# Scores of the two strided attention groups with the keys' high and low parts side by side in one 256-column operand, and one more step at the second strided group's first value projection

## The chip, the cores and the metric

The kernel runs on one core of one Trainium2 chip. The metric is the device time of one execution in microseconds. Four of the core's engines matter here: TensorE (PE in the profile; its weight loads have a row of their own, PEld), VectorE (DVE), ScalarE (ACT) and the DMA queues, of which the ACT queue carries a few small transfers that this change touches.

## What is computed

One layer of a bidirectional encoder on 512 tokens of width 1024, in float32: a SwiGLU feed-forward half step, a token-mixing block, and a second feed-forward half step, each normalised before and after. The change lies in the mixing block, in the branch with twelve heads of 64 features in three groups. Each group is a banded attention over tokens that lie `dilation` apart; the three groups' outputs are then mixed per token and head by a softmax over their log-sum-exps:

```python
DIL_PAIRS = ((128, 1), (512, 4), (2048, 16))
for g, (window, dilation) in enumerate(DIL_PAIRS):
    half = window // (2 * dilation)
    o, lse = _dilated_attention(q[:, :, g], k[:, :, g], v[:, :, g], dilation, half, sl)
    outs.append(o)
    lses.append(lse)
alpha = jax.nn.softmax(jnp.stack(lses, axis=0), axis=0)
o = jnp.stack(outs, axis=0) * alpha[..., None]
```

Inside a group the scores are q·k/8 minus a slope times the distance, and minus infinity outside the band. Group 0 has dilation 1; groups 1 and 2 (dilation 4 and 16) are the strided ones, called far groups in the code. The kernel walks both in the order "token modulo 4", so that 512 tokens become four tiles of 128, and a tile's queries meet only the keys of the same tile.

## The kernel before

**Numbers in two parts.** Nearly every operand of TensorE is split into a high part (a copy of type fp32r, by ScalarE) and a low part (the rest, by VectorE): the helper `split`, lines 111 to 113. A product is then three matmuls, high by high, high by low and low by high (`mm3`, lines 202 to 205). For the scores only 64 features are contracted, so the query's two parts stand one above the other in the 128 partitions (rows `own` high, rows `other` low, line 914), and the key's high part and low part each stand twice, once for each half. Two matmuls then give the whole score: the query tile by `kh`, and the query tile by `kl` added onto it in PSUM.

**`qk_parts`** (line 905) makes those operands for the two heads of a pair from two PSUM banks, `pq` and `pk`: two units of 512 columns for the keys, `kh` and `kl`, with a ScalarE copy and a VectorE subtraction of 512 columns each, and one copy of each into the other 64 partitions.

**`scores`** (line 1025) serves all groups before the change. For group 0 and the neighbourhood branch the windows are wide (256 keys to a query tile), two tiles to a PSUM bank. For the far groups they are narrow (128 keys to a tile, four tiles in one bank), eight matmuls of 128 columns to a head. VectorE then adds the bias table and takes the row minimum of the negated score in one instruction for each tile (line 1041, `tensor_tensor_reduce`), and ScalarE takes the exponential and its sum (line 1046), both with an accumulated result that a second short instruction reads out.

**The order of the work.** TensorE's stream is built by hand. Long projections (24 matmuls) are emitted one after another, and between them a queue `pend` of short pieces of attention is worked off: `step(n)` takes n of them (lines 197 to 200). In the stretch of the change `pend` holds the scores of the far heads, written (g, h) below, and then `joint(1)`. The projections there are: the last pair of query and key projections; `v_far(1)` and `v_far(2)`, two value projections each, copied out of PSUM by ScalarE (line 971); then `v_far(1)`'s eight transposes (line 979); then `v_near`, four groups of 24 matmuls of 256 columns (line 957); then `v_far(2)`'s eight transposes; then sixteen gate projections of 512 columns (line 1294). Before the change a step stands after each of the four value projections, after every second group of transposes, and after each group of `v_near`.

**What hangs on the last scores.** After head 3 of a group its row minima and sums go to DRAM (line 1243, a DMA on the ACT queue). `joint(g)` (line 1221) reads those of all three groups back (line 1224) and works out the mixing weights in about ten short VectorE instructions (lines 1227 to 1236) with one exponential on ScalarE between them (line 1231). `g_tr(g, h)` scales the probabilities by these weights (line 1057) and TensorE transposes them (line 1069). The first of these, `g_tr(1, 0)`, is taken behind the second gate projection.

**The other traffic of VectorE and ScalarE.** Each projection takes one weight piece of 128 by 1024 (two parts) and makes the next one but four be converted: a cast on ScalarE (line 112) and a subtraction on VectorE (line 113). They stand in the same in-order queues as the attention's work. The order within each engine is set by a scheduler at build time, except in stretches that are pinned; the gates' sigmoid and the exponential need different tables on ScalarE, and a table load stands in its queue at each switch.

Of the kernel before, what the change touches and what calls it, by code (L numbers as in the profile page):

```python
# [13 lines left out]
F32R = mybir.dt.float32r  # L14
BF16 = mybir.dt.bfloat16
AF = mybir.ActivationFunctionType
ALU = mybir.AluOpType
# [3 lines left out]
P = 128  # L21
# [24 lines left out]
def block_kernel(ctx, tc, x, gains, weights, rpb_near, rpb_all, alibi0, alibi12, out):  # L46
    nc = tc.nc
# [12 lines left out]
    def unit(dt=F32, name="u"):  # L60
        return up.tile([P, 512], dt, tag="u", name=name)
# [6 lines left out]
    def bank(name="ps"):  # L68
        return pp.tile([P, 512], F32, tag="ps", name=name)
# [41 lines left out]
    def split(hi, lo, src):  # L111
        nc.scalar.copy(hi, src)  # L112
        nc.vector.tensor_tensor(lo, src, hi.bitcast(F32), op=ALU.subtract)  # L113
# [83 lines left out]
    def step(n=1):  # L197
        for _ in range(n):
            if pend:
                pend.popleft()()  # L200
# [671 lines left out]
    def seen(kind, ap):  # L872

        if kind == "na":
            return ap.rearrange("p (r c) -> p c r", r=8)
        if kind == 0:
            return ap
        return ap.rearrange("p (i c) -> p c i", c=4)

    def order_k(kind, ap):  # L880
        if kind == "na":
            return [(slice(0, 128), ap.rearrange("p (r b c) -> p b c r", r=8, b=8)[:, 0:8:7]),
                    (slice(128, 512), ap.rearrange("p (r c) -> p c r", r=8)[:, 8:56])]
        if kind == 0:
            return [(slice(0, 128), ap.rearrange("p (b c) -> p b c", b=8)[:, 0:8:7]),
                    (slice(128, 512), ap[:, 64:448])]
        return [(slice(0, 512), seen(kind, ap))]
# [9 lines left out]
    def shaped(dst, view):  # L897
        sh = view.shape
        if len(sh) == 2:
            return dst  # L900
        if len(sh) == 3:
            return dst.rearrange("p (a b) -> p a b", a=sh[1])
        return dst.rearrange("p (a b c) -> p a b c", a=sh[1], b=sh[2])

    def qk_parts(kind, pq, pk):


        heads = []
        for par in range(2):
            own = slice(par * 64, par * 64 + 64)  # L910
            other = slice(64 - par * 64, 128 - par * 64)
            q, kh, kl = unit(F32R), unit(F32R), unit(F32R)
            v = seen(kind, pq[own])
            qo, qx = shaped(q[own], v), shaped(q[other], v)
            nc.scalar.mul(qo, v, 0.125)
            nc.vector.scalar_tensor_tensor(qx, v, 0.125, qo.bitcast(F32), op0=ALU.mult, op1=ALU.subtract)
            for cols, v in order_k(kind, pk[own]):
                split(shaped(kh[own, cols], v), shaped(kl[own, cols], v), v)
            nc.vector.tensor_copy(kh[other], kh[own].bitcast(F32))
            nc.scalar.copy(kl[other], kl[own].bitcast(F32))  # L920
            heads.append((q, kh, kl))
        return heads
# [39 lines left out]
    def v_far(g):  # L962


        feats = []
        for _ in range(2):
            o = bank()
            proj_into(o, take())
            u = unit(name="vt")
            v = seen(g, o)  # L970
            nc.scalar.copy(shaped(u, v), v)
            feats.append(u)
            step()
        yield
        vv = []
        for n in range(4):
            ps = bank()
            for i, u in enumerate(feats):
                nc.tensor.transpose(ps[:, i * P:(i + 1) * P], u[:, n * P:(n + 1) * P], ident)
            vv.append(v_parts(ps[:, :256]))  # L980
            if n % 2:
                step()
        yield vv

    def v_proj_na():
# [29 lines left out]
                vv[i].append(v_parts(acc[n][:, i * 256:(i + 1) * 256]))  # L1015
        yield vv

    def windows(wide, kT, i):
        if not wide:
            return kT[:, i * P:(i + 1) * P]  # L1020
        if i < 3:
            return kT[:, i * P:i * P + 256]
        return kT.rearrange("p (b c) -> p b c", b=4)[:, 0:4:3]

    def scores(wide, parts, table, st, h):

        q, kh, kl = parts
        w = 256 if wide else 128
        per = 512 // w
        prob = []  # L1030
        for b in range(NT // per):
            ps = bank()
            p = unit()
            for i in range(b * per, (b + 1) * per):
                o = (i - b * per) * w
                cols = slice(i * P, (i + 1) * P)
                nc.tensor.matmul(ps[:, o:o + w], q[:, cols], windows(wide, kh, i), start=True, stop=False)
                nc.tensor.matmul(ps[:, o:o + w], q[:, cols], windows(wide, kl, i), start=False, stop=True)
            for i in range(b * per, (b + 1) * per):
                o = (i - b * per) * w  # L1040
                nc.vector.tensor_tensor_reduce(
                    out=p[:, o:o + w], in0=ps[:, o:o + w], in1=table(i), scale=-1.0, scalar=3.0e38,
                    op0=ALU.add, op1=ALU.min, accum_out=st[:, i, h, 0:1])
            for i in range(b * per, (b + 1) * per):
                o = (i - b * per) * w
                nc.scalar.activation(p[:, o:o + w], p[:, o:o + w], AF.Exp, bias=st[:, i, h, 0:1],
                                     scale=-1.0, accum_out=st[:, i, h, 1:2])
            prob.append(p)
        return prob
# [106 lines left out]
    def mixing(g):  # L1156
        o_parts = [None] * 10
        hold = {}

        def table_of(us, h):  # L1160
            def f(i):
                s = (h % 2) * 3 + (0 if i == 0 else 2 if i == 3 else 1)
                return us[s // 2][:, (s % 2) * 256:(s % 2) * 256 + 256]
            return f
# [20 lines left out]
        na_tab = [[] for _ in range(4)]  # L1185
# [2 lines left out]

        def na_sc(parts, h):
            s4 = sp.tile([P, 4, 1, 2], F32, tag="nast", name="nast", bufs=4)  # L1190
            pr = scores(True, parts[h % 2], table_of(na_tab[h // 2], h), s4, 0)
            rc = sp.tile([P, 4], F32, tag="narc", name="narc", bufs=4)
            nc.vector.reciprocal(rc, s4[:, :, 0, 1])
            scale_probs(True, pr, lambda i: rc[:, i:i + 1])
            hold["p", h] = pr
# [19 lines left out]
        g_tab = {0: [], 1: [], 2: [], 3: []}  # L1215
        st_u = unit(name="st")
        st = [st_u[:, g * 32:g * 32 + 32].rearrange("p (t h c) -> p t h c", t=4, h=4) for g in range(3)]
# [19 lines left out]
            scl[g] = s  # L1237

        def g_sc(g, parts, h):
            tab = table_of(g_tab[h // 2], h) if g == 0 else lambda i: g_tab[g + 1][0][:, h * P:(h + 1) * P]  # L1240
            hold["p", g, h] = scores(g == 0, parts[h % 2], tab, st[g], h)
            if h == 3:
                nc.scalar.dma_start(st_views[g][:, :, 8 * g:8 * g + 8], st[g].rearrange("p t h c -> p t (h c)"))

# [63 lines left out]
        parts = {}  # L1308
        duos = [[None] * 2 for _ in range(2)]
        n0 = total - 3 * NF - NK  # L1310
        o = Blocks(n0, 1, duos)
# [210 lines left out]
    part = small("ms0")  # L1522
# [168 lines left out]
```

## Time and profile before

| | us |
|---|---|
| median of 3 runs (lowest, highest) | 1084.52 (1083.33, 1084.96) |
| the profiled execution | 1084.06 |
| its span, first to last instruction | 1081.9 |
| busy in that span: TensorE | 1074.0 (99%) |
| TensorE's weight loads | 968.4 (90%) |
| VectorE | 834.3 (77%) |
| ScalarE | 658.5 (61%) |

How to read it: the profiled execution has its own time, 2.2 us longer than its span (1084.06 - 1081.9), and 0.5 us under the median of the runs. In the views by time (the timeline), a row has its start, its duration, the engine, the line, the operation with the tile that it writes and those that it reads, its shape, and in square brackets the idle time of the engine before it with what ended it. TensorE's durations overlap: two matmuls that start 0.23 us apart are shown with 0.39 us each, so the price of a matmul in a stream is the distance from its start to the start of the next.

### The profile page before, as it was taken

How to read it: one execution, taken by the hardware profiler on the slowest of the kernel's cores; microseconds unless marked ns; L12 is line 12 of the kernel's file. 1: busy time of each engine (PE TensorE's matmuls, PEld its weight loads, DVE VectorE, ACT ScalarE, POOL GpSimd, SP SyncE). 2: the span in 40 equal slices, each digit the busy share in tenths (PEclk: the TensorE clock that was granted, in tenths of full speed). 3: DMA queues.
4: the chain of work that ended last, by engine and by line, in shares of the span. 5: the costliest groups of instructions: out<-in, count | busy, mean ns of one | idle time of the engine just before them, and what ended most of it. 6: DMA issues, size and time to landing. Idle time of an engine off the chain costs nothing.

```text
span 1081.9 us, 18434 instructions
## 1 busy us (share of the span) xinstructions
PE 1074.0 (99%) x6691; PEld 968.4 (90%) x6691; DVE 834.3 (77%) x1568; ACT 658.5 (61%) x1339; POOL 178.2 (16%) x247
## 2 busy tenths in 40 slices
PE   9999999999999999999999999999999999999997
PEld 7899999998888988888988888889899999998886
DVE  8987777778997679876467654777988777778985
ACT  7645555565784767767656651366656555565762
POOL 3111122014334000000000001133302111104301
PEclk9999999999999999999999999999999999999999
DMA  9888898569993453422232239665928777759962
GB/s 324 194 207 223 218 237 219 143 169 289 236 282 96 128 182 120 136 84 79 74 100 82 78 96 311 159 115 193 292 76 211 193 167 188 197 180 240 217 206 78
DMA packets 95725, 189.82 MB, mean 175 GB/s; under 512 B 24081, under 2 KB 26641, under 8 KB 95634
## 3 DMA queue, kind: packets, MB, share of 16 engines
q1 hardware_dynamic: 68320, 134.18, 37.3%
q0 software_dynamic: 24624, 54.01, 27.7%
q8 instruction: 52, 0.85, 0.3%
q10 hardware_dynamic: 2690, 0.46, 0.2%
q14 instruction: 39, 0.32, 0.1%
HBM read 183.58 MB, written 7.58 MB: 177 GB/s over the span
## 4 chain that ended last, share of the span: by engine, by line
PE 96%; DVE 1%; ACT 1%; DMA 1%; issue 0%; POOL 0%; DVEq 0%; ACTq 0%; POOLq 0%
PE q L203 11%; PE q L204 11%; PE q L205 11%; PE ps L203 11%; PE ps L204 11%; PE ps L205 11%; PE p L203 4%; PE p L204 4%; PE p L205 4%; PE r L205 3%; PE r L203 3%; PE r L204 3%; PE c L204 2%; PE c L205 2%; PE c L203 2%; PE ps L1069 1%
## 5 line engine op out<-in xcount | busy, mean ns | idle before, releaser
L113 DVE TENSOR_TENSOR w<-raw,w 128x512 fp32r<-128x512 f32 (+1 forms) x136 | 122.9, 909 | 70.0 <-ACT w L112 69.8
L112 ACT CAST w<-raw 128x512 fp32r<-128x512 f32 (+1 forms) x136 | 107.9, 801 | 84.9 <-PE ps L204 42.2
L203 PE MATMUL ps<-hn,w 128*128 128x512 f32 (+1 forms) x408 | 155.5, 381 | 0.2
L204 PE MATMUL ps<-hn,w 128*128 128x512 f32 (+1 forms) x408 | 153.2, 376 | 0.2 <-DVE hn L340 0.2
L205 PE MATMUL ps<-hn,w 128*128 128x512 f32 (+1 forms) x408 | 153.2, 375 | 0.0
L112 ACT CAST w<-t 128x512 fp32r<-128x512 f32 x160 | 97.1, 619 | 52.3 <-DVE t L402 29.3
L113 DVE TENSOR_TENSOR w<-t,w 128x512 fp32r<-128x512 f32 x160 | 109.2, 689 | 23.6 <-ACT w L112 20.9
L203 PE MATMUL p<-v,w 128*128 128x256 f32 x320 | 90.6, 283 | 0.0
L204 PE MATMUL p<-v,w 128*128 128x256 f32 x320 | 90.5, 283 | 0.0
L203 PE MATMUL q<-v,w 128*128 128x256 f32 x320 | 90.5, 283 | 0.0
L204 PE MATMUL q<-v,w 128*128 128x256 f32 x320 | 90.4, 283 | 0.0
L205 PE MATMUL p<-v,w 128*128 128x256 f32 x320 | 90.2, 283 | 0.0
L205 PE MATMUL q<-v,w 128*128 128x256 f32 x320 | 89.9, 283 | 0.0
L205 PEld LDWEIGHTS ps<-hn,w 128*128 128x128 f32 x408 | 76.8, 188 | 14.0
L203 PEld LDWEIGHTS ps<-hn,w 128*128 128x128 f32 x408 | 76.9, 189 | 13.2 <-ACT hn L339 0.4
L204 PEld LDWEIGHTS ps<-hn,w 128*128 128x128 f32 x408 | 77.0, 189 | 13.0 <-DVE hn L340 0.5
L396 POOL DMA_DIRECT2D t<-in_weights_dram x40 | 35.0, 874 | 287.0 <-DMA t<-in_weights_dram 124.0
L205 PE MATMUL q<-hn,w 128*128 128x256 f32 x288 | 81.5, 283 | 0.0
L204 PE MATMUL q<-hn,w 128*128 128x256 f32 x288 | 81.5, 283 | 0.0
L203 PE MATMUL q<-hn,w 128*128 128x256 f32 x288 | 81.3, 283 | 0.0
L203 PE MATMUL q<-w,a 128*128 128x512 f32 x192 | 75.0, 391 | 0.2 <-DVE part L851 0.2
L204 PE MATMUL q<-w,a 128*128 128x512 f32 x192 | 74.7, 389 | 0.0
(283 smaller groups left out, 3020.6 us busy)
## 6 DMA issues: line engine op xcount, KB each, us to landing
raw<-in_weights_dram SPq DMA_DIRECT2D x90, 512.0 KB
t<-in_weights_dram SPq DMA_DIRECT2D x88, 256.0 KB
t<-in_weights_dram POOLq DMA_DIRECT2D x80, 256.0 KB, 5.5
w<-in_weights_dram SPq DMA_DIRECT2D x40, 256.0 KB
rows<-in_weights_dram SPq DMA_DIRECT2D x32, 256.0 KB
w<-in_weights_dram POOLq DMA_DIRECT2D x32, 256.0 KB, 6.6
tb<-in_weights_dram POOLq DMA_DIRECT2D x12, 512.0 KB, 8.0
rows<-in_weights_dram POOLq DMA_DIRECT2D x24, 256.0 KB, 10.2
```

What stands on the lines that cost most here:

```text
L112: nc.scalar.copy(hi, src)
L113: nc.vector.tensor_tensor(lo, src, hi.bitcast(F32), op=ALU.subtract)
L203: nc.tensor.matmul(o, sh, mh, start=start, stop=False, **kw)
L204: nc.tensor.matmul(o, sh, ml, start=False, stop=False, **kw)
L205: nc.tensor.matmul(o, sl, mh, start=False, stop=stop, **kw)
L396: nc.gpsimd.dma_start(t1, weights[gate][:, :512], accum_op=ALU.add)
L1069: nc.tensor.transpose(ps[:, i * P:(i + 1) * P], s, ident)
```

## The change

Three things, all in the mixing block:

1. For the far groups `qk_parts` no longer makes one unit of high parts and one of low parts. Each of the two key units now holds two tiles' 256 high columns and then the same tiles' 256 low columns. So the copy and the subtraction of 512 columns become two copies and two subtractions of 256.
2. A new function, `scores_narrow`, replaces `scores` for the far groups. A query tile meets its 128 high and 128 low key columns in one matmul of 256 columns, taken as two runs of 128 that lie 256 columns apart. The two products lie side by side in PSUM instead of being added there. A head fills two PSUM banks with two matmuls each. VectorE first adds the low products of two tiles to the bias table (`low`, 128 by 256), and the row minimum then adds the high product to that.
3. The steps: `v_far(2)` takes two steps behind its first projection instead of one, and the steps between the transposes of both `v_far` are gone.

```diff
             q, kh, kl = unit(F32R, "q"), unit(F32R, "k"), unit(F32R, "k")
...
-            for cols, v in order_k(kind, pk[own]):
-                split(shaped(kh[own, cols], v), shaped(kl[own, cols], v), v)
+            if kind in (1, 2):
+                v = seen(kind, pk[own])
+                for i, u in enumerate((kh, kl)):
+                    part = v[:, 2 * i:2 * i + 2]
+                    split(shaped(u[own, :256], part), shaped(u[own, 256:], part), part)
+            else:
+                for cols, v in order_k(kind, pk[own]):
+                    split(shaped(kh[own, cols], v), shaped(kl[own, cols], v), v)
...
-        for _ in range(2):
+        for i in range(2):
             o = bank()
             proj_into(o, take())
...
-            step()
+            step(2 if (g, i) == (2, 0) else 1)
...
             vv.append(v_parts(ps[:, :256]))
-            if n % 2:
-                step()
...
+    def scores_narrow(parts, table, st, h):
+
+        q, ks = parts[0], parts[1:]
+        p = unit()
+        for b in range(2):
+            ps = bank()
+            for i in range(2):
+                k = ks[b].rearrange("p (s n t) -> p n s t", s=2, n=2)[:, i]
+                nc.tensor.matmul(ps[:, i * 256:(i + 1) * 256], q[:, (2 * b + i) * P:(2 * b + i + 1) * P], k,
+                                 start=True, stop=True)
+            low = unit(name="low")
+            o = ps.rearrange("p (n s t) -> p n s t", n=2, s=2)
+            nc.vector.tensor_tensor(low[:, :256].rearrange("p (n t) -> p n t", n=2), o[:, :, 1],
+                                    table.unsqueeze(1).to_broadcast([P, 2, P]), op=ALU.add)
+            for n in range(2):
+                i = 2 * b + n
+                nc.vector.tensor_tensor_reduce(
+                    out=p[:, i * P:(i + 1) * P], in0=o[:, n, 0], in1=low[:, n * P:(n + 1) * P], scale=-1.0,
+                    scalar=3.0e38, op0=ALU.add, op1=ALU.min, accum_out=st[:, i, h, 0:1])
+            for i in (2 * b, 2 * b + 1):
+                s = slice(i * P, (i + 1) * P)
+                nc.scalar.activation(p[:, s], p[:, s], AF.Exp, bias=st[:, i, h, 0:1], scale=-1.0,
+                                     accum_out=st[:, i, h, 1:2])
+        return [p]
...
-            hold["p", g, h] = scores(g == 0, parts[h % 2], tab, st[g], h)
+            if g == 0:
+                hold["p", g, h] = scores(parts[h % 2], table_of(g_tab[h // 2], h), st[g], h)
+            else:
+                hold["p", g, h] = scores_narrow(parts[h % 2], g_tab[g + 1][0][:, h * P:(h + 1) * P], st[g], h)
```

The lines below `qk_parts` have other numbers in the changed kernel: the scores' product is L1035, the sum with the table L1039, the row minimum L1043, its exponential L1048, the value transposes L985, the transfers of `stats` and `joint` L1271 and L1250, joint's instructions L1253 to L1262, the scaling L1083, the probabilities' transposes L1095 and the sigmoid L1324.

The order of the instructions on each engine, at three places. First TensorE around `v_far(1)`'s transposes. Before, head (1,3) stands between the two halves of the transposes (L979), as eight products of 128 columns:

```order
L979 MATMUL ps<-ident,vt 128x128 x4
L1037 MATMUL ps<-u 128x128
L1038 MATMUL ps<-u 128x128
L1037 MATMUL ps<-u 128x128
L1038 MATMUL ps<-u 128x128
L1037 MATMUL ps<-u 128x128
L1038 MATMUL ps<-u 128x128
L1037 MATMUL ps<-u 128x128
L1038 MATMUL ps<-u 128x128
L979 MATMUL ps<-ident,vt 128x128 x4
```

Now the head (1,3) stands ahead of all eight transposes, as four products, and the first matmuls of `v_near` follow at once:

```order
L205 MATMUL ps<-hn,w 128x512
L1035 MATMUL ps<-k,q 128x256 x4
L985 MATMUL ps<-ident,vt 128x128 x8
L203 MATMUL ps<-w,hn 128x256
L204 MATMUL ps<-w,hn 128x256
```

Heads (1,1) and (1,2) now follow each other behind `v_far(2)`'s first projection, (2,0) to (2,3) stand behind the first to the fourth group of `v_near` (before, (2,3) stood behind the third), and `joint(1)` comes after `v_far(2)`'s transposes. Of the first four probability transposes, before all ahead of the third gate, TensorE now does one ahead of that gate and three behind its nineteenth matmul.

Second, ScalarE from the last exponentials to the first of `joint`. `w<-raw` is the cast of a weight piece, `u<-ps` a part of the values, `stats` and `joint` are the transfers to and from DRAM. Before:

```order
L1046 ACTIVATE u,st<-u,st 128x128 x4
L112 CAST w<-raw 128x1024
L1243 DMA stats<-st 512x1x8
L112 CAST u<-ps 128x4x64
L112 CAST w<-raw 128x1024
L1224 DMA joint<-stats 128x96
L112 CAST u<-ps 128x4x64 x4
L1231 ACTIVATE joint<-joint 128x48
```

Now, from the last two exponentials of head (2,2) on (the `x4` are those of head (2,3)):

```order
L1048 ACTIVATE u,st<-u,st 128x128 x2
L112 CAST u<-ps 128x4x64
L112 CAST w<-raw 128x1024
L112 CAST u<-ps 128x4x64 x4
L1048 ACTIVATE u,st<-u,st 128x128 x4
L1271 DMA stats<-st 512x1x8
L112 CAST w<-raw 128x1024
L1250 DMA joint<-stats 128x96
L1324 ACT_TABLE_LOAD
L1324 ACTIVATE sig<-ps 128x512
L1257 ACT_TABLE_LOAD
L1257 ACTIVATE joint<-joint 128x48
```

The casts of a weight piece and of five value parts, which stood behind the last exponentials, now stand ahead of them, and the first gate's sigmoid with two table loads has come between the reading of `joint` and its exponential.

Third, VectorE at head (2,3). `ISA u,st` is the row minimum, `ISA st` its short second instruction. Before:

```order
L1041 ISA u,st<-ps,table 128x128
L1041 ISA st 128x1
L113 TENSOR_TENSOR w<-raw,w 128x1024
L113 TENSOR_TENSOR u<-ps,u 128x4x64
L113 TENSOR_TENSOR w<-raw,w 128x1024
L113 TENSOR_TENSOR u<-ps,u 128x4x64 x2
L1227 TENSOR_TENSOR joint<-joint 128x16
```

Now, from the second sum with the table on:

```order
L1039 TENSOR_TENSOR low<-ps,table 128x256
L113 TENSOR_TENSOR w<-raw,w 128x1024
L113 TENSOR_TENSOR u<-ps,u 128x4x64 x2
L1043 ISA u,st<-ps,low 128x128
L1043 ISA st 128x1
L1043 ISA u,st<-ps,low 128x128
L1043 ISA st 128x1
L113 TENSOR_TENSOR u<-ps,u 128x4x64 x2
L113 TENSOR_TENSOR w<-raw,w 128x1024
L1253 TENSOR_TENSOR joint<-joint 128x16
```

A weight subtraction and two value parts now stand between the head's last `low` and its last two row minima, and another weight subtraction ahead of `joint`'s first instruction; one more, not shown, stands ahead of the head's first `low`. SyncE's and GpSimd's orders are the same as before.

More of the change, by code (lines that the diff above doesn't have):

```diff
@@ L911, in qk_parts @@
             other = slice(64 - par * 64, 128 - par * 64)
-            q, kh, kl = unit(F32R), unit(F32R), unit(F32R)
+            q, kh, kl = unit(F32R, "q"), unit(F32R, "k"), unit(F32R, "k")
             v = seen(kind, pq[own])
@@ L1016, in v_proj_na, with windows @@
         yield vv
-    def windows(wide, kT, i):
-        if not wide:
-            return kT[:, i * P:(i + 1) * P]
+    def windows(kT, i):
         if i < 3:
@@ L1023, in windows, with scores @@
         return kT.rearrange("p (b c) -> p b c", b=4)[:, 0:4:3]
-    def scores(wide, parts, table, st, h):
+    def scores_narrow(parts, table, st, h):
[21 more added lines that the diff above has]
+        return [p]
+    def scores(parts, table, st, h):
         q, kh, kl = parts
-        w = 256 if wide else 128
-        per = 512 // w
+        w, per = 256, 2
         prob = []
@@ L1036, in scores @@
                 cols = slice(i * P, (i + 1) * P)
-                nc.tensor.matmul(ps[:, o:o + w], q[:, cols], windows(wide, kh, i), start=True, stop=False)
-                nc.tensor.matmul(ps[:, o:o + w], q[:, cols], windows(wide, kl, i), start=False, stop=True)
+                nc.tensor.matmul(ps[:, o:o + w], q[:, cols], windows(kh, i), start=True, stop=False)
+                nc.tensor.matmul(ps[:, o:o + w], q[:, cols], windows(kl, i), start=False, stop=True)
             for i in range(b * per, (b + 1) * per):
@@ L1190, in na_sc @@
             s4 = sp.tile([P, 4, 1, 2], F32, tag="nast", name="nast", bufs=4)
-            pr = scores(True, parts[h % 2], table_of(na_tab[h // 2], h), s4, 0)
+            pr = scores(parts[h % 2], table_of(na_tab[h // 2], h), s4, 0)
             rc = sp.tile([P, 4], F32, tag="narc", name="narc", bufs=4)
@@ L1239, in g_sc @@
         def g_sc(g, parts, h):
-            tab = table_of(g_tab[h // 2], h) if g == 0 else lambda i: g_tab[g + 1][0][:, h * P:(h + 1) * P]
-            hold["p", g, h] = scores(g == 0, parts[h % 2], tab, st[g], h)
+            if g == 0:
+                hold["p", g, h] = scores(parts[h % 2], table_of(g_tab[h // 2], h), st[g], h)
+            else:
+                hold["p", g, h] = scores_narrow(parts[h % 2], g_tab[g + 1][0][:, h * P:(h + 1) * P], st[g], h)
             if h == 3:
```

## Prediction

> **What bounds the kernel now.** I read the page's head and its chain first, then the waits of TensorE, then the windows around the change, last the timelines. The page:
>
> ```profile
> span 1081.9 us, 18434 instructions
> ...
> PE 1074.0 (99%) x6691; PEld 968.4 (90%) x6691; DVE 834.3 (77%) x1568; ACT 658.5 (61%) x1339; POOL 178.2 (16%) x247
> ...
> PEclk9999999999999999999999999999999999999999
> ...
> PE 96%; DVE 1%; ACT 1%; DMA 1%; issue 0%; POOL 0%; DVEq 0%; ACTq 0%; POOLq 0%
> ```
>
> TensorE is busy 99% of the span, the chain that ended last is TensorE's for 96%, and the clock is full in every slice. All waits of TensorE on other engines are three rows, 1.6 us together:
>
> ```profile
> PE warm L1470 <- DVE idle L1435: 1.2, 1, 1.2
> PE ps L204 <- DVE hn L340: 0.2, 1, 0.2
> PE q L203 <- DVE part L851: 0.2, 1, 0.2
> ```
>
> None stands at the attention. In the window that holds two of the strided heads TensorE is full too, while VectorE is busy 7.38 of 10 us (columns: TensorE, weight loads, VectorE, ScalarE, GpSimd, clock, DMA share, GB/s):
>
> ```profile
> 530.00:540.00 10.00, 10.00 (x88) 10.00 (x86) 7.38 (x47) 9.35 (x47) 0.00 (x0) 1.00 0.20 57
> ```
>
> So a shorter TensorE stream shortens the time, as long as no new wait arises. Two sums decide: what TensorE saves, and how late `joint(1)` becomes.
>
> **TensorE's saving.** A wide head (eight products of 256 columns) and a narrow head (eight of 128), each with the long matmul behind it:
>
> ```profile
> 508.35 0.28 PE L1037 MATMUL ps<-u 128*128 128x256 f32 x1
> ...
> 509.07 0.28 PE L1037 MATMUL ps<-u 128*128 128x256 f32 x1
> 509.19 0.28 PE L1038 MATMUL ps<-u 128*128 128x256 f32 x1
> 509.31 0.40 PE L203 MATMUL ps<-hn,w 128*128 128x512 f32 x1
> 509.54 0.40 PE L204 MATMUL ps<-hn,w 128*128 128x512 f32 x1
> ...
> 514.77 0.22 PE L1037 MATMUL ps<-u 128*128 128x128 f32 x1
> ...
> 515.62 0.45 PE L203 MATMUL ps<-hn,w 128*128 128x512 f32 x1
> 515.91 0.40 PE L204 MATMUL ps<-hn,w 128*128 128x512 f32 x1
> ```
>
> Eight products of 128 take 514.77 to 515.62, 0.85 us (0.11 each), and the next long matmul holds TensorE 0.29 (515.62 to 515.91) where behind the wide head it holds it 0.23 (509.31 to 509.54): 0.91 us in all. Eight products of 256 take 508.35 to 509.31, 0.96 us: 0.12 each, hardly more than one of 128. So four of 256 should take 0.48, and a head saves 0.43. Eight heads: 3.4 us. The after-effect of 0.06 was not paid by (1,2) and (1,3), which transposes followed, so 3.3. The new operand is read in two runs of 128 columns; the price I use already covers that, since the last window of the wide head (509.07 to 509.19, 0.12) is also read in two pieces (both ends: 0.12, or 0.24 if each run cost a product of its own).
>
> A rule on this: the Trainium skill, "TensorE: Matmul & The Clock Gate", section "Back-to-back issue gap", gives some 0.081 us per matmul of 128 columns in a stream with weight loads and N/2.4 + 2.5 ns, 0.109 at 256, for an isolated one. By these figures eight heads would save 8 x (8 x 0.081 - 4 x 0.109) = 1.7 us, not 3.4. The row of 128 columns (0.11) disagrees with the page, that of 256 (0.12) is near it; I go by the rows.
>
> The steps also break the first four probability transposes in two, 1 and 3, with one more switch from a long product to transposes and back. Before, one such group stands here (with the end of head (2,3), the first product behind it, and when the probability transposes are first asked for):
>
> ```profile
> 542.32 0.33 PE L203 MATMUL ps<-w,u 128*128 128x256 f32 x1
> ...
> 545.25 1.04 PE L979 MATMUL ps<-ident,vt 128*128 128x128 f32 x8
> 546.04 0.47 PE L203 MATMUL ps<-hn,w 128*128 128x512 f32 x1
> 546.35 0.39 PE L204 MATMUL ps<-hn,w 128*128 128x512 f32 x1
> ...
> 557.03 0.60 PE L1069 MATMUL ps<-ident,u 128*128 128x128 f32 x4
> ```
>
> The product behind transposes holds TensorE 0.31 (546.04 to 546.35) instead of 0.23: 0.1 lost. Net saving without waits: 3.2 us.
>
> **What is hidden.** VectorE gets sixteen `low` instructions. No row shows one; the nearest is a VectorE instruction on 128x256 read from PSUM (546.62 below), 0.33 from start to start; ends 0.28, a row minimum of half the width, and 1.0, nearly that of 1024 columns. I take 0.33, that of the same size: 16 x 0.33 = 5.3 us of VectorE beside a TensorE that is full while VectorE has 2.6 of 10 us idle. Cost nothing, except in the chain below. The eight copies and eight subtractions of 512 columns that become sixteen and sixteen of 256 add some fixed parts, 0.1 to 0.2 us each, on engines with idle time there; nothing if the next heads' operands are still a projection ahead, as they were.
>
> **`joint(1)`, the new wait.** Here the change uses up spare time. Before, the chain from (2,3)'s products (542.32) to the first scaled probabilities ends at 551.8 to 552.1, and TensorE asks for them at 557.03: about 5 us spare. Now (2,3) stands 24 products later, and the queues of VectorE and ScalarE that it passes through have moved too. VectorE's rows (start and duration; the bracket is the idle time before):
>
> ```profile
> 538.75 0.29 DVE L1041 CUSTOM_DVE_ANT_0 u<-ps,table 128x128 f32<-128x128 f32 x1 [1.66 <-PE ps L1038]
> ...
> 538.96 0.28 DVE L1041 CUSTOM_DVE_ANT_0 u<-ps,table 128x128 f32<-128x128 f32 x1
> ...
> 546.62 0.42 DVE L113 TENSOR_TENSOR u<-ps,u 128x256 fp32r<-128x256 f32 x1
> 546.95 1.22 DVE L113 TENSOR_TENSOR w<-raw,w 128x1024 fp32r<-128x1024 f32 x1
> 548.08 0.75 DVE L113 TENSOR_TENSOR u<-ps,u 128x256 fp32r<-128x256 f32 x2
> 549.02 0.18 DVE L1227 TENSOR_TENSOR joint<-joint 128x16 f32<-128x16 f32 x1 [0.18 <-DMA joint<-stats]
> ...
> 549.78 0.17 DVE L1228 TENSOR_TENSOR joint<-joint 128x16 f32<-128x16 f32 x1
> ...
> 550.63 0.21 DVE L1232 TENSOR_TENSOR joint<-joint 128x48 f32<-128x48 f32 x1 [0.31 <-ACT joint L1231]
> ...
> 551.79 0.88 DVE L1057 TENSOR_SCALAR u<-u,joint 128x128 f32<-128x128 f32 x4
> ```
>
> and ScalarE's with its DMA issues:
>
> ```profile
> 544.02 0.39 ACT L1046 ACTIVATE u<-u,st 128x128 f32<-128x128 f32 x1
> ...
> 544.41 1.03 ACT L112 CAST w<-raw 128x1024 fp32r<-128x1024 f32 x1
> 544.53 0.52 ACTq L1243 DMA_DIRECT2D stats<-st  x1
> 545.45 0.37 ACT L112 CAST u<-ps 128x256 fp32r<-128x256 f32 x1
> 545.71 1.05 ACT L112 CAST w<-raw 128x1024 fp32r<-128x1024 f32 x1
> 546.64 0.37 ACTq L1224 DMA_DIRECT2D joint<-stats  x1
> ...
> 550.35 0.24 ACT L1231 ACTIVATE joint<-joint 128x48 f32<-128x48 f32 x1 [2.10 <-DVE joint L1230]
> ...
> 552.63 1.28 ACT L1296 ACT_TABLE_LOAD   x1
> 553.93 0.60 ACT L1296 ACTIVATE sig<-ps 128x512 f32<-128x512 f32 x1
> ```
>
> From start to start: value part 0.33 (546.62 to 546.95), weight subtraction 1.13 (to 548.08), row minimum 0.21, exponential 0.39, weight cast 1.04 (544.41 to 545.45), value cast 0.26. I add these in the new order, with zero where the first `low` of head (2,2) starts, which is when its first two products are done (0.12 + 0.28 = 0.40 after its start):
>
> - TensorE: `v_near`'s last group starts at 0.48 - 0.40 = 0.1 and takes 542.32 to 545.25, 2.9; (2,3) 0.5, its first two products done at about 3.4; eight transposes 0.8 (545.25 to 546.04); two gates 11.0 (546.04 to 557.03). The scaled probabilities are asked for at 15.2.
> - VectorE, (2,2): `low` 0, value part, minima 0.7 and 0.9, `low` 1.1, minima to 2.1. ScalarE: two exponentials from 1.1, weight cast 1.8 to 2.9, two exponentials, value cast, weight cast 3.8 to 4.9, value casts 4.8 to 5.9.
> - VectorE then waits for the first cast: subtraction 2.9 to 4.1, so (2,3)'s first `low` starts at 4.1 instead of 3.4. Value part 4.4, minima 4.7 and 4.9, `low` 5.2, weight subtraction 5.5, two value parts 6.6 and 7.0, the last minima 7.3 and 7.5, done at 7.9.
> - ScalarE: exponentials 7.7 and 8.1, done with their read-out at 8.7; `stats` is issued; the read of `joint` follows 2.1 later (544.53 to 546.64), 10.8; `joint`'s first instruction 2.4 after that (546.64 to 549.02), 13.2.
> - The exponential of `joint` stood 1.33 behind it (549.02 to 550.35), with two value parts (0.67) between, which are now ahead: 0.7 to 0.8, so 14.0. In its queue the sigmoid with two table loads starts behind the read's issue: 10.9 + 1.3 + 0.6 + 1.3 = 14.1, level with it.
> - From the exponential to the scaling 1.44 (550.35 to 551.79): 15.5, and the first scaled tile 0.2 to 0.3 later, 15.8.
>
> Asked for at 15.2, there at 15.8: TensorE waits 0.6 us. If VectorE took the minima of (2,3) at once when its products are done, the chain would be 2 us or more shorter and nothing would be waited for; if the queues run another 0.6 late, which is as much as one cast that slips behind a value part or two, it is 1.2. So 0 to 1.2, and I take the sum, 0.6. Other probability transposes come behind this one and find their tiles scaled 0.2 apart.
>
> Total: 3.2 - 0.6 = 2.6 us less. The profiled execution took 1084.06 us (2.2 outside its span): 1081.5. The median shown is 0.5 higher, so on its scale 1081.9.
>
> **Rivals.**
>
> - *The wait is wholly covered.* The scheduler's order hides the weight subtractions or the DMA pair comes back faster. For it: the sum misses by only 0.6 of 15. Against: three in-order queues have to be on time. Full saving, 3.3: 1081.2.
> - *The chain is 1.5 to 3 us late.* Each stop (the cast, the DMA pair, the table loads) may slip, and the level pair at 14.1 leaves no slack. The saving shrinks to between 1.2 and 0: 1083.3 to 1084.5. Against: the durations are rows of the same engines, a few us away.
> - *Slower: `low` is dear.* It reads PSUM in two pieces and a table repeated by a stride of nothing. Per group of `v_near` (24 x 0.12 + 0.48 = 3.4 us) VectorE has two `low`, four minima, a value part and a weight subtraction: 0.66 + 0.84 + 0.33 + 1.13 = 3.0. From a `low` of 0.85 us VectorE is the slower engine; at 1.0 it is 4.3, 0.9 behind per group, 3.7 in four groups; the wait grows to 4.3, and with 3.2 saved the kernel loses 1.1: 1085.6. Against: the value parts, also read from PSUM in pieces, take the 0.33 of a plain instruction.
> - *The merge saves nothing.* If two runs make two matmuls of it, a head is 8 x 0.12 and the time stays: 1084.5. Against: the row 509.07.
> - *A dear table load.* The Trainium skill, "ScalarE: Activation LUTs", section "What ACT_TABLE_LOAD costs", counts a drain behind the load, about 2.7 us together. As a mechanism here: if each of the two loads held ScalarE twice as long as its row of 1.28, the exponential of `joint` would start at 10.9 + 2.6 + 0.6 + 2.6 = 16.7, 2.6 later, the wait would be 3.2 and the gain gone: 1084.5. Against: the sigmoid starts 1.30 behind the load (552.63 to 553.93).
>
> **How the numbers follow.** Forecast 0.53 (the wait 0 to 1.2, so 1081.3 to 1082.5), covered wait 0.20, late chain 0.15, dear `low` 0.05, no merge 0.04, dear table load 0.03. About 0.2%, 2.2 us, is what a measurement of this kernel can tell from no change; from 1084.5 that is anything under 1082.3. The covered wait and most of the forecast lie under it (0.20 + 0.45): faster 0.65. The rest of the forecast, the late chain, the last two rivals and the mildest cases of the dear `low` lie within: 0.29. Slower 0.06, the dear `low` and what I have not thought of. The range runs from the covered wait with a little more saved, 1080.7, to the middle of the late chain, 1083.9.
>
> **What would show it.** In the changed profile: four products of 256 columns 0.12 apart at L1035, and the next long product 0.48 behind the first; `low` (L1039) at 0.33 from start to start; a new row in TensorE's waits at L1095 on VectorE's L1083 of about 0.6 us; on ScalarE the exponential of `joint` (L1257) right behind a table load. The forecast is wrong if the scores' products are 0.2 apart, if TensorE shows a wait at other lines, such as those of `v_near` or the gates, or if the wait at L1095 is over 2 us.

## The result and the profile after

The changed kernel takes 1081.38 us (median of 11 runs, 1080.16 to 1082.32) against 1083.99 us before (11 runs, 1083.33 to 1084.96): ratio 0.9975, 95% interval 0.9967 to 0.9983, so 2.6 us less. The forecast was 1081.9 us, 2.6 us under before. The profiled execution took 1081.67 us at a span of 1079.9.

Not all of the 2.6 us lies in the span from the first to the last instruction. The kernel before takes 2.1 to 2.2 us beyond its span in every execution; the changed kernel and all kernels of the experiments below, the one with the old scores too, take 1.7 to 1.9. So 0.4 of the 2.6 us lies outside the span, where neither TensorE's saving nor the wait can show, and 2.2 lies inside it. No run shows what the 0.4 comes from. The differences to before given below all contain it.

All waits of TensorE in the changed kernel (total, times, longest):

```profile
PE warm L1498 <- DVE idle L1463: 1.2, 1, 1.2
PE ps L1095 <- DVE u L1083: 0.9, 1, 0.9
PE q L205 <- DVE a L113: 0.4, 1, 0.4
PE q L203 <- DVE part L851: 0.4, 1, 0.4
PE ps L204 <- DVE hn L340: 0.2, 1, 0.2
PE ps L203 <- ACT hn L339: 0.2, 1, 0.2
```

The second row is the new wait that was forecast, at the forecast place: the first probability transposes wait for their scaling. The rows of `q` and `hn` lie in the feed-forward halves; their size changed from one profile to the next (the row of `part` from 0.2 to 1.0 us) in kernels that do not touch those halves, and nothing here rests on them.

A narrow head on TensorE, now with the long matmul behind it:

```profile
514.86 0.64 PE L1035 MATMUL ps<-k,q 128*128 128x256 f32 x4
515.33 0.40 PE L203 MATMUL ps<-hn,w 128*128 128x512 f32 x1
515.56 0.40 PE L204 MATMUL ps<-hn,w 128*128 128x512 f32 x1
```

Four products take 514.86 to 515.33, 0.47 us, and the long matmul behind them holds TensorE 0.23. Before it was 0.85 and 0.29. So a head saves 0.44 (1.14 against 0.70).

VectorE from head (2,2)'s first `low`, the zero of the forecast's sum, to the scaling:

```profile
538.59 0.42 DVE L1039 TENSOR_TENSOR low<-ps,table 128x256 f32<-128x256 f32 x1 [1.31 <-PE ps L1035]
538.93 0.41 DVE L113 TENSOR_TENSOR u<-ps,u 128x256 fp32r<-128x256 f32 x1
...
541.44 1.23 DVE L113 TENSOR_TENSOR w<-raw,w 128x1024 fp32r<-128x1024 f32 x1 [0.80 <-ACT w L112]
542.58 0.42 DVE L1039 TENSOR_TENSOR low<-ps,table 128x256 f32<-128x256 f32 x1
...
551.13 0.17 DVE L1253 TENSOR_TENSOR joint<-joint 128x16 f32<-128x16 f32 x1 [0.51 <-DMA joint<-stats]
...
551.54 0.35 DVE L1256 TENSOR_TENSOR joint<-joint 128x16 f32<-128x16 f32 x3
553.26 0.21 DVE L1258 TENSOR_TENSOR joint<-joint 128x48 f32<-128x48 f32 x1 [1.37 <-ACT joint L1257]
...
554.42 2.83 DVE L1083 TENSOR_SCALAR u<-u,joint 128x128 f32<-128x128 f32 x14
```

A `low` costs 0.34 from start to start (538.59 to 538.93). Head (2,3)'s first one starts at 542.58, when the weight subtraction is through, as in the sum. Between the last subtraction of `joint` (551.54, three in 0.35) and the next VectorE row stands an idle time of 1.37 us, ended by ScalarE. ScalarE in that stretch:

```profile
547.03 0.52 ACTq L1271 DMA_DIRECT2D stats<-st  x1
548.30 1.05 ACT L112 CAST w<-raw 128x1024 fp32r<-128x1024 f32 x1 [1.30 <-PE ps L204]
549.41 0.34 ACTq L1250 DMA_DIRECT2D joint<-stats  x1
549.78 1.28 ACT L1324 ACT_TABLE_LOAD   x1 [0.42 <-DMA stats<-st]
551.08 0.60 ACT L1324 ACTIVATE sig<-ps 128x512 f32<-128x512 f32 x1
551.69 1.28 ACT L1257 ACT_TABLE_LOAD   x1
552.99 0.24 ACT L1257 ACTIVATE joint<-joint 128x48 f32<-128x48 f32 x1
```

The exponential's operand is there at 551.9, but ScalarE is still in the sigmoid and the table load for the exponential; it starts at 552.99. And the first transpose:

```profile
554.85 0.30 PE L1095 MATMUL ps<-ident,u 128*128 128x128 f32 x1 [0.92 <-DVE u L1083]
```

### The profile page after: what moved, and what is told of

Its sections match the earlier page's. It is cut to its first block, busy times and chain, and to the rows that moved or that the text cites. A ratio compares the mean times of both kernels' runs of the same rounds, so it can differ in the third digit from the quotient of the medians.

```text
span 1079.9 us, 18417 instructions
## 1 busy us (share of the span) xinstructions
PE 1070.5 (99%) x6659; PEld 964.8 (89%) x6659; DVE 841.3 (78%) x1592; ACT 662.8 (61%) x1349; POOL 178.9 (17%) x247
## 4 chain that ended last, share of the span: by engine, by line
PE 96%; DVE 2%; DMA 1%; ACT 1%; issue 1%; SPq 0%; POOL 0%; DVEq 0%; ACTq 0%; POOLq 0%
PE q L205 11%; PE q L203 11%; PE q L204 11%; PE ps L204 11%; PE ps L203 11%; PE ps L205 11%; PE p L203 4%; PE p L204 4%; PE p L205 4%; PE r L205 3%; PE r L203 3%; PE r L204 3%; PE c L205 2%; PE c L204 2%; PE c L203 2%; PE ps L1095 1%
```

## The experiments

Theory: a head saves 0.43 us because a product costs the same at 128 and at 256 columns, and the new steps cost a wait at `joint(1)`. Rivals: the steps bring part of the gain themselves; the saving comes from no longer adding up in PSUM; the wait has another cause than the queues of VectorE and ScalarE.

**The steps undone** (new scores, old steps):

```diff
-            step(2 if (g, i) == (2, 0) else 1)
+            step()
...
             vv.append(v_parts(ps[:, :256]))
+            if n % 2:
+                step()
```

> The new scores with the steps where they stood before. Theory (the merged products save 3.3 us of TensorE, and the new steps cost a wait of 0.9 us at the first probability transposes and one more break in the stream): head (2,3) stands one group of v_near earlier again, joint's exponential follows the first joint instructions without table loads between, the wait at the probability transposes is gone, so 3.3 us under the kernel before, 0.7 us or so under the changed kernel. Rival (the new steps bring a part of the gain, because heads no longer stand among the transposes): less saved than the changed kernel's 2.6 us, 2 or under.

Measured: 1082.46 us against 1083.91, ratio 0.9986 (0.9977 to 0.9994): 1.5 us saved, not 3.3 (inside the span 1.1). The theory failed here, and the rival's number held. The wait at the probability transposes was gone, as expected, but another was there. TensorE and VectorE of this kernel, heads (1,2), (1,3) and (2,0):

```profile
526.92 0.64 PE L1037 MATMUL ps<-k,q 128*128 128x256 f32 x4
527.40 0.60 PE L985 MATMUL ps<-ident,vt 128*128 128x128 f32 x4
527.75 0.72 PE L1037 MATMUL ps<-k,q 128*128 128x256 f32 x4
528.31 0.60 PE L985 MATMUL ps<-ident,vt 128*128 128x128 f32 x4
528.66 0.48 PE L1037 MATMUL ps<-k,q 128*128 128x256 f32 x2
530.70 0.47 PE L1037 MATMUL ps<-k,q 128*128 128x256 f32 x2 [1.55 <-DVE st L1045]
```

```profile
528.25 0.42 DVE L1041 TENSOR_TENSOR low<-ps,table 128x256 f32<-128x256 f32 x1
528.58 1.22 DVE L113 TENSOR_TENSOR w<-raw,w 128x1024 fp32r<-128x1024 f32 x1
529.71 0.42 DVE L1041 TENSOR_TENSOR low<-ps,table 128x256 f32<-128x256 f32 x1
530.05 0.28 DVE L1045 CUSTOM_DVE_ANT_0 u<-ps,low 128x128 f32<-128x128 f32 x1
...
530.25 0.29 DVE L1045 CUSTOM_DVE_ANT_0 u<-ps,low 128x128 f32<-128x128 f32 x1
```

In the code the pool of PSUM tiles has eight banks; I count them as handed out in turn. From (1,2) on they go: two for (1,2), two for transposes, two for (1,3), two for transposes; (2,0) takes the ninth and the tenth. The tenth is (1,2)'s second, and its last minimum ends at 530.5, behind a weight subtraction and the `low` of (1,3). (2,0)'s third product starts at 530.70, and the row names that minimum's line as what it waited for. So with two banks to a head the old steps don't fit, and the new steps avoid a wait of 1.55 us. That it is the bank is read from these rows; the run that was to test it came out unclear (two tiles in one bank, below). Inside the span 2.2 of the 3.3 us are missing, and the wait is 1.55 of them; the rest was not followed up.

**The steps alone** (the scores of before with the new steps):

```diff
-        for _ in range(2):
+        for i in range(2):
...
-            step()
+            step(2 if (g, i) == (2, 0) else 1)
...
-            if n % 2:
-                step()
```

> The scores of before with the new steps. Theory: TensorE's work is that of before, with one more break; without the sums with the table VectorE hands head (2,3) on about 1 us earlier and TensorE asks 0.4 us later, so the wait of 0.9 us shrinks to 0 to 0.2; together 0 to 0.4 us slower than before. Rival (the steps bring a part of the gain): 0.8 us or more faster than before.

Measured: 1084.17 against 1083.91, ratio 1.0003 (0.9994 to 1.0012). The time is what the theory said: the steps bring no gain of their own. The wait at the probability transposes was 0.5 us, more than the 0.2 expected. The four combinations are then: old scores 0 with the old steps and +0.3 with the new ones, new scores -1.5 with the old steps and -2.6 with the new ones. Inside the span they are 0, +0.6, -1.1 and -2.2; the 0.6 of the steps alone is about the wait of 0.5 and the 0.1 that was forecast for one more switch. The two parts are worth more together than apart.

**Two products instead of one of 256 columns:**

```diff
-                k = ks[b].rearrange("p (s n t) -> p n s t", s=2, n=2)[:, i]
-                nc.tensor.matmul(ps[:, i * 256:(i + 1) * 256], q[:, (2 * b + i) * P:(2 * b + i + 1) * P], k,
-                                 start=True, stop=True)
+                for s in range(2):
+                    k = ks[b][:, s * 256 + i * P:s * 256 + (i + 1) * P]
+                    nc.tensor.matmul(ps[:, i * 256 + s * P:i * 256 + (s + 1) * P],
+                                     q[:, (2 * b + i) * P:(2 * b + i + 1) * P], k, start=True, stop=True)
```

> The changed kernel, but each query tile meets its high and its low key columns in two products of 128 columns, written side by side. Theory (a product costs about 0.11 to 0.12 us whether it has 128 or 256 columns): a head takes 0.85 to 0.91 us again, 3.2 to 3.4 us more than the changed kernel; TensorE asks for the probabilities 0.4 us later, so the wait shrinks to 0.5; 2.8 to 3.2 us slower than the changed kernel, level with before or up to 0.5 slower. Rival (the saving comes from no longer adding up in PSUM): within 0.5 us of the changed kernel.

Measured: 1085.06 against 1083.91, ratio 1.0008 (0.9999 to 1.0017), 1.2 us slower than before where the changed kernel is 2.6 faster. A head on TensorE:

```profile
515.43 1.00 PE L1036 MATMUL ps<-k,q 128*128 128x128 f32 x8
516.27 0.45 PE L203 MATMUL ps<-hn,w 128*128 128x512 f32 x1
```

Eight products take 0.84 us, as before the change, though none of them is added onto another in PSUM. Not adding up in PSUM saves nothing; merging does. The time came out 0.7 us beyond the expected limit; the wait at the probability transposes was 1.1 us here instead of 0.5. What the rows show for it is `stats`: from its sending to the read of `joint` it took 3.1 us (550.48 to 553.58), where the changed kernel took 2.4 (547.03 to 549.41). That is the 0.6 us and a little more.

**Four products of 64 columns** (as the kernel above, each half split again):

```diff
-                for s in range(2):
+                for s in range(4):
...
```

> As the kernel with two products of 128 columns for each query tile, but with four of 64 columns. Theory (a product of up to 256 columns costs its start-to-start distance of 0.11 to 0.12 us whatever its columns, so that only the number of products counts): sixteen products take 1.8 us a head instead of 0.9, 7 us slower than the kernel with two products, near 1092. Rival (a product costs by its columns, and 128 to 256 happens to be flat): 0.06 us each, within 1 us of that kernel.

Measured: 1092.47 against 1083.76, ratio 1.0073 (1.0057 to 1.0088). A head on TensorE:

```profile
514.40 1.87 PE L1036 MATMUL ps<-k,q 128*128 128x64 f32 x16
516.10 0.48 PE L203 MATMUL ps<-hn,w 128*128 128x512 f32 x1
```

The theory held. Sixteen products take 514.40 to 516.10, 1.70 us. So a product costs 0.11 us at 64 columns (1.70 / 16), 0.11 at 128 (0.84 / 8) and 0.12 at 256 (0.47 / 4): the number of products counts, up to 256 columns.

**The exponential of `joint` ahead of the first sigmoid** (a dependence that only orders ScalarE's queue):

```diff
             nc.scalar.activation(e, e, AF.Exp)
+            hold["exp", g] = list(nc.cur_bb.bb.instructions)[-1]
...
             nc.scalar.activation(s, o, AF.Sigmoid)
+            if not sig:
+                tc.add_manual_dep(list(nc.cur_bb.bb.instructions)[-1], hold["exp", 1].name, mybir.DependencyInfo(
+                    mybir.DependencyClass.NoSync, mybir.DependencyReason.DATA), reason="program order")
```

> The changed kernel with the first gate's sigmoid held, on ScalarE, behind the exponential of joint, so that no table load stands between the reading of joint and that exponential. Theory (the pair of table loads and the sigmoid in ScalarE's queue make the last microsecond of the chain): joint's exponential starts about 1.0 us earlier, the wait of 0.9 us at the probability transposes goes to 0 to 0.2, 0.7 to 0.9 us faster than the changed kernel, 3.4 us under before. Rival (the data of joint come last, the table loads lie beside that): the wait stays at 0.7 us or more, within 0.2 us of the changed kernel.

Measured: 1080.17 against 1083.72, ratio 0.9965 (0.9952 to 0.9978), 3.6 us under before. All of TensorE's waits are now

```profile
PE warm L1502 <- DVE idle L1467: 1.2, 1, 1.2
PE ps L204 <- DVE hn L340: 0.2, 1, 0.2
PE ps L203 <- ACT hn L339: 0.2, 1, 0.2
```

and on ScalarE the exponential starts as soon as VectorE's part is there:

```profile
548.64 0.34 ACTq L1250 DMA_DIRECT2D joint<-stats  x1
551.29 0.25 ACT L1257 ACTIVATE joint<-joint 128x48 f32<-128x48 f32 x1 [2.70 <-DVE joint L1256]
```

From the read's issue to the exponential it is 2.65 us (548.64 to 551.29) instead of 3.58 (549.41 to 552.99): 0.9 us, the whole wait, as the theory said. The table loads were the last link of the chain.

**The sum with the table twice**, in all heads and in (2,3) alone (`again` is true for that head):

```diff
+            nc.vector.tensor_tensor(low[:, 256:].rearrange("p (n t) -> p n t", n=2), o[:, :, 1],
+                                    table.unsqueeze(1).to_broadcast([P, 2, P]), op=ALU.add)
...
+            if again:
+                nc.vector.tensor_tensor(low[:, 256:].rearrange("p (n t) -> p n t", n=2), o[:, :, 1],
+                                        table.unsqueeze(1).to_broadcast([P, 2, P]), op=ALU.add)
```

> The changed kernel with every sum with the table done twice, the second into columns that nothing reads. Theory (VectorE's queue lies on the chain to joint, so that a lengthening shows one for one in the wait): 3 to 4 more instructions of 0.33 us lie ahead of head (2,3)'s last exponentials, the wait at the probability transposes grows from 0.9 to between 1.9 and 2.2, 1.0 to 1.3 us slower than the changed kernel. Rival (the wait comes from the DMA pair and the table loads alone, VectorE has room): no difference, within 0.3 us.

> The changed kernel with the sum with the table done twice in head (2,3) alone. In the order of the queues that is two instructions of 0.33 us more on VectorE and one value part that now stands ahead of the last minima, 1.0 us; and on ScalarE the weight cast, which waits for TensorE until 548.3 in the changed kernel and took 1.05, now stands ahead of the sending of stats instead of behind it. Theory (every instruction that stands ahead in an in-order queue counts, one that waits for another engine most): stats is sent at about 549.4 instead of 547.0, the wait of 0.9 us grows by 2.3 to about 3.2, 2.3 us slower than the changed kernel, level with before. Rival (only VectorE's own lengthening counts): 1.0 us slower than the changed kernel. Second rival (the chain has room): no difference.

In all heads: 1089.47 against 1083.91, ratio 1.0055 (1.0041 to 1.0069), 8.1 us above the changed kernel. Both theories missed, because the order changed as well. Its ScalarE:

```profile
548.02 1.05 ACT L112 CAST w<-raw 128x1024 fp32r<-128x1024 f32 x1 [2.49 <-PE ps L204]
548.97 0.40 ACT L1050 ACTIVATE u<-u,st 128x128 f32<-128x128 f32 x1
...
549.88 0.52 ACTq L1273 DMA_DIRECT2D stats<-st  x1
553.87 0.34 ACTq L1252 DMA_DIRECT2D joint<-stats  x1
554.24 1.28 ACT L1326 ACT_TABLE_LOAD   x1 [4.38 <-DMA stats<-st]
...
558.87 0.24 ACT L1259 ACTIVATE joint<-joint 128x48 f32<-128x48 f32 x1
```

A weight cast that had to wait 2.49 us for TensorE's products now stood ahead of (2,3)'s last exponentials, `stats` took 4.0 us to be read back (549.88 to 553.87) instead of 2.4, and a second sigmoid and a cast stood between the table loads. TensorE waited 7.1 us instead of 0.9, and its clock fell (below). Why `stats` took longer stays open: in other runs here it took anything from 2.1 to 4.1 us. So this run doesn't price a `low`.

In (2,3) alone: 1082.81 against 1083.76, ratio 0.9989 (0.998 to 0.9997); the changed kernel on the same chip had 0.9972 (next paragraph), and by the two medians this kernel is 1.7 us slower. The wait was 2.0 us instead of 0.9 and 0.7, so it grew by 1.1 to 1.3. Counted from (2,2)'s first `low`, (2,3)'s last minimum starts 1.0 us later than in the changed kernel (8.4 against 7.4) and `joint`'s exponential 1.1 (15.5 against 14.4). So the lengthening of VectorE's queue came through about one for one, as the first rival said; the 0.4 to 0.6 us by which the time grew more than the wait are not explained. The theory's 2.3 was too much:

```profile
548.55 1.05 ACT L112 CAST w<-raw 128x1024 fp32r<-128x1024 f32 x1 [0.30 <-PE ps L204]
548.61 0.52 ACTq L1274 DMA_DIRECT2D stats<-st  x1
```

The sending of `stats` is issued 0.06 behind the start of the cast ahead of it, not behind its end. The cast in the queue cost about its own wait, 0.3, and not its 1.05.

**The changed kernel once more:**

> The changed kernel once more, on the same chip as the kernels of this call. Theory: 2.2 to 3.1 us under before, with the wait of 0.6 to 1.1 us at the probability transposes as its only new one in the mixing block. Rival (the difference of the first comparison was partly the chip's): under 1.5 us.

Measured: 1081.1 against 1083.76, ratio 0.9972 (0.9961 to 0.9982), with a wait of 0.7 us at L1095. The first comparison stands. `stats` took 2.2 us to be read back here and 2.4 in the first profile, which is the difference between the two waits.

**The probability transposes one gate later:**

```diff
-            if f:
+            if f > 1:
                 step(2)
```

> The changed kernel with the probability transposes begun one gate later (the two steps behind the second gate are left out, the rest is worked off behind the last gate). Theory (the wait of 0.9 us is all that the later joint costs): the wait goes, 0.7 to 0.9 us faster than the changed kernel unless the pieces left for the end cost as much there. Rival (the wait is given back elsewhere, or the same chain is waited for again): within 0.3 us of the changed kernel, or slower.

Measured: 1082.43 against 1083.72, ratio 0.9988 (0.9979 to 0.9996): 1.3 us faster than before, less than the changed kernel. The rival held: the wait for the scaling went, and another came where the rest is worked off:

```profile
626.64 0.66 PE L1095 MATMUL ps<-ident,u 128*128 128x128 f32 x4 [1.60 <-DVE u L1136]
```

L1136 adds up attended values out of PSUM; with the pieces crowded at the end, transposes wait 1.6 us for its bank.

**The far heads one place earlier** (one more step behind `v_far(1)`'s second projection):

```diff
-            step(2 if (g, i) == (2, 0) else 1)
+            step(2 if (g, i) in ((1, 1), (2, 0)) else 1)
```

> The changed kernel with a second step behind the second projection of the first far group, so that all later heads stand one place earlier, head (2,3) behind the third group of v_near as before. Theory: no three heads stand within a few microseconds, so no bank is waited for, and joint has its 3.4 us more, so the wait at the probability transposes goes: 0.8 to 0.9 us faster than the changed kernel, 3.2 to 3.5 under before. Rival (two pairs of heads in a row make VectorE late, and a bank or the joint is waited for again): 0 to 1 us slower than the changed kernel.

Measured: 1080.18 against 1083.72, ratio 0.9964 (0.9952 to 0.9976), 3.5 us under before, with no wait of TensorE in the mixing block, as the theory said. This version and the one with the ordered exponential are the fastest; the two can't be told apart. Their intervals overlap the changed kernel's, so that they are faster than it rests on the rows: the wait of 0.9 us is gone.

**Two tiles' value transposes in one bank**, with the old steps:

```diff
         for n in range(4):
-            ps = bank()
+            if n % 2 == 0:
+                both = bank()
+            ps = both[:, n % 2 * 256:n % 2 * 256 + 256]
```

> The new scores with the steps where they stood before (the kernel whose head (2,0) waited 1.6 us), but the value transposes of two tiles share a PSUM bank, so that they take two banks instead of four. Theory (a narrow head takes two of the eight banks instead of one, and with three heads among the transposes the ninth bank asked for is still being read by VectorE): the third product of (2,0) no longer waits for a minimum of (1,2), 1.4 to 1.6 us faster than that kernel, 3.0 to 3.3 under before. Rival (VectorE is simply late there, whichever bank is asked for): the wait stays over 1 us, within 0.4 us of that kernel.

Measured: 1088.17 (1084.75 to 1089.96) against 1083.72, ratio 1.0036 (1.0023 to 1.005). Heads (1,2), (1,3) and (2,0) went through without a wait, as the theory said. But half of the transposes were now ordered between later heads, whose products waited for banks that still held values:

```profile
532.89 0.51 PE L1039 MATMUL ps<-k,q 128*128 128x256 f32 x2 [0.92 <-DVE u L113]
```

A second such wait took 0.7 us, and three at the probability transposes 1.3 together. The profiled execution took 1084.75, the others 2.4 to 5.2 us more, and no trace shows why. As a test of the banks it is inconclusive: the order of TensorE changed with it.

## Why the prediction was right

**TensorE's saving.** Forecast 0.43 a head and 3.2 us in all. The rows give 0.44, and the two versions without a wait in the mixing block are 3.5 and 3.6 us under before, inside the span 3.2 each. The step was right: a product of 256 columns costs hardly more than one of 128, also when it reads two runs. The merge rival fell by the row at 514.86. The 1.7 us that followed from the figures of the Trainium skill are half of that. An explanation that fits the flat price is in the Trainium skill, "TensorE: Matmul & The Clock Gate", section "LDWEIGHTS (loading the stationary operand)": P/1.2, which gives 107 ns for a load of 128 columns. The products of 64 columns, 0.106 us apart, agree with that figure. The rows of the weight loads themselves do not: one takes 0.19 us in these profiles, overlapping the next. That the weight load is the cause was not tried by itself.

**The wait.** Forecast 0.6 at L1095, measured 0.9 and 0.7. From zero at 538.59, forecast and measured: (2,3)'s first `low` 4.1 and 3.99, `stats` 8.7 and 8.44, the read 10.8 and 10.82, `joint`'s first instruction 13.2 and 12.54, its exponential 14.1 and 14.40, the scaling 15.5 and 15.83, the first scaled tile 15.8 and 16.26; TensorE asked for it at 15.2 and 15.34. The agreement at the read is luck: `stats` was sent 0.3 earlier than summed, and the way from there to the read took 2.4 instead of 2.1. Two later terms were mis-sized. The way from the read to `joint`'s first instruction was taken as 2.4 from before; it is 1.7. In both profiles VectorE stood idle just before that instruction until the read had landed (0.18 us before, 0.51 now), so it is the transfer itself that was shorter; why, no run shows. And the table load starts 0.37 behind the read's issue, not 0.1. So the two arms that the sum had level were not: VectorE's was ready at 551.9 and ScalarE's at 552.99, and the table loads alone set the end, as the run with the ordered exponential showed. The rivals on both sides, the covered wait and the late chain, did not happen.

**`low` and the table loads.** 0.34 against 0.33 forecast; the point of 0.85 from which it would have decided was far off. The exponential starts 1.30 behind its table load (551.69 to 552.99), so the rival of the dear load fell too.

**What the prediction did not see.** It counted the new steps as a cost only, 0.1 and the wait. The run with the old steps showed that they also pay: without them 1.55 us go to a wait for the tenth bank. The forecast of the whole came out because in the changed kernel no bank is waited for, not because the steps were understood; that part is luck.

**The total.** That the forecast met the 2.6 us to the tenth is luck too. Inside the span, where all its terms lie, the gain was 2.2: the saving of 3.2 was right and the wait 0.3 longer than summed. The 0.4 outside the span, which the prediction carried over unchanged from before, made up for it.

## What to carry to other kernels

Count products, not columns, where they are short, here up to 256 columns: two of 128 columns that share the stationary operand cost nearly twice one of 256 (0.21 against 0.12 us). When a piece of work takes more banks, follow the ring of banks through the densest stretch before the pieces are reordered. And where an instruction on a chain needs another table than its neighbours in ScalarE's queue, look which of them stands ahead: ordering one sigmoid behind it was worth a wait of 0.9 us. Where a gain is a few tenths of a per cent, compare the spans as well as the times.

## What the runs showed of the hardware that was not expected

While TensorE waited for 7.1 us in the kernel with the doubled sums, its granted clock fell to 0.50, and it came back only some 5 us after TensorE had work again (the last three numbers are the clock, the DMA share and GB/s):

```profile
554.00:556.00 2.00, 0.00 (x0) 0.00 (x0) 0.32 (x2) 1.75 (x2) 0.00 (x0) 0.91 0.10 25
556.00:558.00 2.00, 0.00 (x0) 0.00 (x0) 1.28 (x5) 1.98 (x4) 0.00 (x0) 0.50 0.00 0
...
564.00:566.00 2.00, 2.00 (x6) 1.59 (x5) 0.00 (x0) 0.00 (x0) 0.00 (x0) 0.53 0.00 0
566.00:568.00 2.00, 2.00 (x12) 1.64 (x11) 0.00 (x0) 0.08 (x1) 0.00 (x0) 1.00 0.00 0
```

The waits of up to 2.0 us left it at 1.00. Of that kernel's 8.1 us, 6.2 are the longer wait. The other 1.9 are of the size of what the clock costs: TensorE worked from 560.7 to about 566 at half speed, an estimate of up to 2.6 us. The run doesn't separate the two further.

The two small transfers on the chain to `joint` did not take the same time in every kernel. From the sending of `stats` to the read of `joint` it was 2.1 us in the kernel before and 4.1 in the one with the steps undone, where ScalarE stood idle for it for 3.35. From the read to `joint`'s first instruction it was 1.7 in the changed kernel and 2.7 in the one with the far heads one place earlier. No run shows what sets these times, and a wait of 0.6 us can't be forecast closer than they vary.
